# Loads at the changes of pair in product order, h ahead of w_out, and the two heads' value products side by side

## The chip, the cores and the metric

One core of a Trainium2 chip. The metric is device time in microseconds (us) of one launch. TensorE does the matmuls, VectorE and ScalarE the elementwise work, GpSimd little; SyncE (SP) issues all the large transfers, on one queue and in program order. Each engine works through its own list in order and waits at semaphores for the others.

## The reference, cut to what matters

4096 tokens of width 1024, one layer, all float32:

```
proj = x @ w_in                       # 1024 -> 3584 columns
xa, ba, ca, u, v, xc, da, dg, q, gate = split(proj)
y_a = ba * conv3(ca * xa)             # short gated convolution
y_b = spatial_gating(u, v)
y_c = multiscale_pool(xc)
y_d = silu(layer_norm(conv31(da * sigmoid(dg)))) @ w_pw
k, v = split(mem @ w_kv)              # 256 memory rows, 4 heads of 64
y_e = softmax(q k^T / 8) v            # per head
h = concat(y_a .. y_e) * silu(gate)   # width 1280
x = layer_norm(alpha * x + h @ w_out)
```

## The kernel before, in words

**Tiling.** The 4096 tokens are eight blocks of 512, worked as four pairs. For each pair (`p`) the input projection makes all 3584 columns, in 14 sets that `mpair` (L226) computes one after the other; between them stand the five branches, whose results are multiplied by their gates and written to DRAM as `h`. After the fourth pair comes the output stage: 32 chunks of 128 tokens, `h @ w_out` and the layer norm (the loop near the end, matmuls at L758).

**Products.** `mpair` computes a 2x2 block product (two blocks of tokens by two chunks of columns, the inner dimension in two halves) by seven products in place of eight: PA, PT1, PT2, PB, PT3, PD, PT4, in this order. Their x side are seven sums and differences of the four quarters b11, b12, b22, b21 of the pair's x. Each is kept as a high and a low part, so that a product is 12 matmuls of 128x512: for k = 0 to 3 the low part by the high weights (L210), the high part by the low weights (L212), the high by the high (L213). Each x tile has two halves along k, `kap` 0 (k 0 and 1) and `kap` 1 (k 2 and 3), so a product needs both. The results go through PSUM banks `mm`; PT1's and PT2's are read by VectorE's adds `t` and `v` (L91), the later ones by the adds to `cc`. The sixth product, PD, needs a bank that the `t` add has read.

**x_prep** (L122) makes these 28 tiles, which have one place each: eight loads of 512 KB (`load`, L131) to `xraw`, eight subtractions in place (`sub`, L94), and for each of the fourteen halves `split_to`: ScalarE casts to the high part (L87), VectorE subtracts for the low part (L88). A tile of the next pair can be written when the last product of the old pair that reads its place is done. So the change of pair falls into the last `mpair` of the old pair and the first of the new one. For the first pair all eight loads are in flight at once. For the later pairs the code goes half by half: four loads of kap 0 and seven steps, then four loads of kap 1 and seven steps; all eight use the four `raw` slots, so that the loads of kap 1 wait for steps of kap 0.

**The filter.** The 31-tap convolution (`d_conv`, L463) of a pair is 60 steps on VectorE, on two accumulators, fed out bit by bit (`take`) while the next pair's first sets run. `d_tail` then takes the result; it begins with transposes on TensorE (L429).

**Attention** (`attention`, L599) runs 16 times: four pairs, two groups of heads (`i`), two blocks (`n`). Queries are cast (L594) and subtracted, scores for two heads `j` are made on TensorE (L608), the exponentials scaled, and each head's 128x512 is transposed in two parts `mc` (four transposes each, L628), copied out by ScalarE (L631, `pT`) and multiplied by the values (L633). A value product has 64 columns, one half of the array: head 0 writes partitions 0 to 63 of `po`, head 1 partitions 64 to 127.

**The last change.** After the fourth pair the 28 places of the x tiles are given out again, in the order in which the products free them (`free`, `place`). `w_out` comes as ten tiles of 512 KB (`woraw`, L706), each split into two places; then `lng` and `lnb`; and `htags`, the six places of `h`, are the last six. `load_h(0)` (loads at L726) loads and splits the first 256 rows of `h`.

**Order.** The program is written once in Python, and each engine's list, SP's too, is put in order by a scheduler.

Of the kernel before, what the change touches and what calls it, by code (L numbers as in the profile page):

```python
# [11 lines left out]
F32 = mybir.dt.float32  # L12
# [10 lines left out]
T = 512  # L23
# [4 lines left out]
NKO = DMIX // P  # L28
# [24 lines left out]
def trunk(ctx, tc, a, out):  # L53
    nc = tc.nc
# [10 lines left out]
    def nm(s):  # L65
        uid[0] += 1
        return f"{s}_{uid[0]}"
# [5 lines left out]
    def tt(tag, dt=F32, n=None):  # L73
        cols, bufs = SLOTS[tag]
        return (wp if tag == "ws" else tp).tile([P, cols], dt, tag=tag, name=nm(n or tag), bufs=bufs)
# [10 lines left out]
    def split_to(hi, lo, src):  # L86
        nc.scalar.copy(out=hi, in_=src)  # L87
        nc.vector.tensor_tensor(out=lo, in0=src, in1=hi.bitcast(F32), op=ALU.subtract)  # L88
# [4 lines left out]
    def sub(dst, x, y):  # L93
        nc.vector.tensor_tensor(out=dst, in0=x, in1=y, op=ALU.subtract)  # L94
# [27 lines left out]
    def x_prep(p):  # L122

        xs = [[None, None] for _ in range(7)]
        raws = {}

        def put(i, kap, src):
            xs[i][kap] = x_place(i, kap)
            split_to(*xs[i][kap], src)

        def load(kap, j, n):  # L131
            tag = "big" if p == 0 and kap == 1 else "raw"
            raw = tt(tag, n="xraw")[:, :2 * T].rearrange("p (k t) -> p k t", k=2)
            k0 = 4 * j + 2 * kap
            nc.sync.dma_start(out=raw, in_=a["xT"][:, k0:k0 + 2, (2 * p + n) * T:(2 * p + n + 1) * T])
            raws[kap, j, n] = raw

        def step(kap, i):
            b11, b12, b22, b21 = (raws.get((kap, *q)) for q in ((0, 0), (0, 1), (1, 1), (1, 0)))
            if i == PT1:  # L140
                sub(b11, b12, b11)
            elif i == PT2:
                sub(b11, b22, b11)
            elif i == PT3:
                sub(b12, b22, b12)
            elif i == PT4:
                sub(b21, b21, b11)
            put(i, kap, {PA: b11, PT1: b11, PT2: b11, PB: b21, PT3: b12, PD: b22, PT4: b21}[i])

        if p == 0:  # L150
            for q in ((0, 0), (0, 1), (1, 1), (1, 0)):
                for kap in range(2):
                    load(kap, *q)
                yield
            for i in range(7):
                for kap in range(2):
                    step(kap, i)
                yield
        else:
            for kap in range(2):  # L160
                for q in ((0, 0), (0, 1), (1, 1), (1, 0)):
                    load(kap, *q)
                for i in range(7):
                    step(kap, i)
        yield xs

# [168 lines left out]
    vm = const([P, 2, 256])  # L335
# [263 lines left out]
    def attention(p, i, n, src, g):  # L599
        q = queries(src)  # L600
        es = [tt("big", n="e")[:, :2 * T].rearrange("p (c m) -> p c m", c=NC4) for _ in range(2)]
        for c2 in range(2):
            sc = [bank(pa, "ax").rearrange("p (c m) -> p c m", c=2) for _ in range(2)]
            for c in range(2):
                t0 = (2 * c2 + c) * P
                for j in range(2):
                    for r, k in enumerate((k1, k2)):
                        nc.tensor.matmul(out=sc[j][:, c], lhsT=q[:, j, t0:t0 + P], rhs=k[i][:, j],  # L608
                                         start=(r == 0), stop=(r == 1))
            for j in range(2):  # L610
                mx = sp.tile([P, 2], F32, tag="mx", name=nm("mx"))
                nc.vector.tensor_reduce(out=mx, in_=sc[j], axis=AX.X, op=ALU.max, negate=True)  # L612
                e = es[j][:, 2 * c2:2 * c2 + 2]
                su = sp.tile([P, 2], F32, tag="su", name=nm("su"))
                for c in range(2):
                    nc.scalar.activation(out=e[:, c], in_=sc[j][:, c], func=AF.Exp, bias=mx[:, c:c + 1],  # L616
                                         accum_out=su[:, c:c + 1])
                ri = sp.tile([P, 2], F32, tag="ri", name=nm("ri"))
                nc.vector.reciprocal(out=ri, in_=su)
                for c in range(2):  # L620
                    nc.vector.tensor_scalar(out=e[:, c], in0=e[:, c], scalar1=ri[:, c:c + 1], scalar2=None,
                                            op0=ALU.mult)
        po = bank(pa, "ax")
        for j in range(2):
            for mc in range(2):
                pt = bank(pa, "ax")
                for c in range(NC4):
                    nc.tensor.transpose(out=pt[:, P * c:P * c + P], in_=es[j][:, c, P * mc:P * mc + P],  # L628
                                        identity=ident)
                pT = tt("wk", n="pT")[:, :T]  # L630
                nc.scalar.copy(out=pT, in_=pt)  # L631
                hd = 2 * i + j
                nc.tensor.matmul(out=po[64 * j:64 * j + 64], lhsT=vm[:, mc, 64 * hd:64 * hd + 64], rhs=pT,  # L633
                                 start=(mc == 0), stop=(mc == 1))
        nc.vector.tensor_tensor(out=g, in0=po, in1=g, op=ALU.mult)
        store(2 * p + n, 8 + i, g)

# [27 lines left out]
    for p in range(NPAIR):  # L665
# [15 lines left out]
        for i in range(2):  # L681
            q, ge = mpair(xs)
# [15 lines left out]
    free = [xc_tag for i in range(7) for kap in range(2) for s in "hl" for xc_tag in (f"x{i}{kap}{s}",)]  # L698

    def place(dt=F32R, n="wo"):  # L700
        return xc.tile([P, 2 * T], dt, tag=free.pop(0), name=nm(n))

    wo = []
    for k in range(NKO):
        raw = tt("raw", n="woraw")
        nc.sync.dma_start(out=raw, in_=a["w_out"][k])  # L706
        wo.append((place(), place()))
        split_to(*wo[k], raw)
    lng, lnb = place(F32, "lng"), place(F32, "lnb")
    nc.sync.dma_start(out=lng, in_=a["ln_g"])  # L710
    nc.sync.dma_start(out=lnb, in_=a["ln_b"])
    htags = free[:6]

    def load_h(u):

# [16 lines left out]
                for k in range(NKO)]  # L732

    hn = load_h(0)
    for b in range(NB):
        for c in range(NC4):
            r0 = b * T + c * P
            if c % 2 == 0:
                hh = hn
            elif r0 < SEQ - P:  # L740
                if r0 == (SEQ - 2 * T) - P:
                    take(conv, 60)
                    d_tail(NPAIR - 1, accs)
                hn = load_h((r0 + P) // 256)
            take(conv, 3)
            r = [tt("cc", n="r") for _ in range(2)]
            for n in range(2):
                nc.sync.dma_start(out=r[n], in_=a["x"][r0:r0 + P, T * n:T * n + T])
            st = sp.tile([P, 2, 6], F32, tag="st2", name=nm("st2"))
            ps = [bank(pm, "mm") for _ in range(2)]  # L750
            steps = [(n, k) for k in range(NKO) for n in range(2)]
            if r0 == SEQ - P:
                steps.sort()
            for n, k in steps:
                hi, lo = hh[k]
                whi, wlo = wo[k]
                for l, ww in ((lo, whi), (hi, wlo), (hi, whi)):
                    nc.tensor.matmul(out=ps[n], lhsT=l[:, P * (c % 2):P * (c % 2) + P], rhs=ww[:, T * n:T * n + T],  # L758
                                     start=(k == 0 and l is lo), stop=(k == NKO - 1 and ww is whi and l is hi))
            for n in range(2):  # L760
                nc.vector.scalar_tensor_tensor(out=r[n], in0=r[n], scalar=ALPHA, in1=ps[n],  # L761
                                               op0=ALU.mult, op1=ALU.add)
                nc.vector.bn_stats(out=st[:, n], in_=r[n])
            mv = sp.tile([P, 2], F32, tag="mv2", name=nm("mv2"))
            nc.vector.bn_aggr(out=mv, in_=st)
            rs = sp.tile([P, 1], F32, tag="rs2", name=nm("rs2"))
            rstd_of(rs, mv[:, 1:2], 1, EPS)
            for n in range(2):
                nc.vector.scalar_tensor_tensor(out=r[n], in0=r[n], scalar=mv[:, 0:1], in1=lng[:, T * n:T * n + T],
                                               op0=ALU.subtract, op1=ALU.mult)  # L770
                nc.vector.scalar_tensor_tensor(out=r[n], in0=r[n], scalar=rs, in1=lnb[:, T * n:T * n + T],
                                               op0=ALU.mult, op1=ALU.add)
                nc.sync.dma_start(out=out[r0:r0 + P, T * n:T * n + T], in_=r[n])
# [59 lines left out]
```

## Time and profile before

| what | value |
|---|---|
| median of 3 runs | 1776.53 us (1776.23 to 1777.87) |
| profiled execution, its own time | 1778.75 us |
| its span | 1777.0 us, mean granted clock 0.993 |
| TensorE busy (PE) | 1728.5 us, 97% |
| VectorE busy (DVE) | 1334.4 us, 75% |
| ScalarE busy (ACT) | 506.6 us, 29% |
| chain that ended last | PE 87%, DVE 7%, DMA 3% |

Busy time is the sum over an engine's instructions, as a share of the span. The chain is the work that ended last, followed back from the last instruction. The granted clock is the share of TensorE's full clock that the chip let it run at: 1.00 is 2.4 GHz, 0.50 is 1.2 GHz. Matmul records have modelled ends, so the distance from one start to the next tells more than the length of one: 0.227 us here for a 128x512 matmul.

### The profile page before, as it was taken

How to read it: one execution, taken by the hardware profiler on the slowest of the kernel's cores; microseconds unless marked ns; L12 is line 12 of the kernel's file. 1: busy time of each engine (PE TensorE's matmuls, PEld its weight loads, DVE VectorE, ACT ScalarE, POOL GpSimd, SP SyncE). 2: the span in 40 equal slices, each digit the busy share in tenths (PEclk: the TensorE clock that was granted, in tenths of full speed). 3: DMA queues.
4: the chain of work that ended last, by engine and by line, in shares of the span. 5: the costliest groups of instructions: out<-in, count | busy, mean ns of one | idle time of the engine just before them, and what ended most of it. 6: DMA issues, size and time to landing. Idle time of an engine off the chain costs nothing.

```text
span 1777.0 us, 21764 instructions
## 1 busy us (share of the span) xinstructions
PE 1728.5 (97%) x7912; PEld 1379.6 (78%) x7912; DVE 1334.4 (75%) x2461; ACT 506.6 (29%) x937; POOL 46.2 (3%) x87
## 2 busy tenths in 40 slices
PE   5999999989999999999999999999989999999997
PEld 4888777878877787887778788777868888888786
DVE  8678887799966539997653999766379996665765
ACT  4323644420144423013532411354241011000300
POOL 0000000000100001010000011000000000000000
PEclk9999999999999999999999999999999999999999
DMA  7767555776754467675446766544683344332621
GB/s 277 264 248 262 199 196 191 286 245 214 239 165 139 130 228 271 203 233 181 131 147 220 265 210 220 198 144 143 207 289 105 115 137 147 125 101 83 213 72 48
DMA packets 128091, 332.79 MB, mean 187 GB/s; under 512 B 14064, under 2 KB 36080, under 8 KB 127984
## 3 DMA queue, kind: packets, MB, share of 16 engines
q1 hardware_dynamic: 127984, 331.39, 55.1%
q8 instruction: 63, 1.03, 0.2%
q14 instruction: 44, 0.36, 0.1%
HBM read 238.02 MB, written 93.32 MB: 186 GB/s over the span
## 4 chain that ended last, share of the span: by engine, by line
PE 87%; DVE 7%; DMA 3%; issue 1%; ACT 1%; SPq 0%; DVEq 0%; ACTq 0%
PE mm L758 24%; PE mm L210 18%; PE mm L213 18%; PE mm L212 18%; PE ax L633 3%; DVE xl L88 2%; PE ax L608 2%; PE ax L628 2%; DVE xraw L94 2%; DMA xraw<-in_xT 1%; PE ax L578 1%; PE ax L429 1%; DVE w L88 1%; PE ax L486 0%; PE ax L476 0%
## 5 line engine op out<-in xcount | busy, mean ns | idle before, releaser
L210 PE MATMUL mm<-xl,w 128*128 128x512 f32 x1568 | 620.4, 396 | 27.5 <-DVE xl L88 21.3
L212 PE MATMUL mm<-xh,w 128*128 128x512 f32 x1568 | 617.2, 394 | 0.9 <-DVE w L88 0.9
L213 PE MATMUL mm<-xh,w 128*128 128x512 f32 x1568 | 615.9, 393 | 0.0
L758 PE MATMUL mm<-wo,h 128*128 128x512 f32 x1920 | 439.8, 391 | 7.5 <-DVE h L88 7.5
L758 PEld LDWEIGHTS mm<-wo,h 128*128 128x128 f32 x1920 | 361.1, 188 | 82.9 <-DVE h L88 8.4
L210 PEld LDWEIGHTS mm<-xl,w 128*128 128x128 f32 x1568 | 296.2, 189 | 94.8 <-DVE xl L88 26.6
L213 PEld LDWEIGHTS mm<-xh,w 128*128 128x128 f32 x1568 | 296.1, 189 | 63.5 <-issue 3.6
L212 PEld LDWEIGHTS mm<-xh,w 128*128 128x128 f32 x1568 | 296.5, 189 | 61.6 <-issue 2.5
L463 DVE SCALAR_TENSOR_TENSOR acc<-din,c,acc 128x1024 f32<-128x1024 f32 x240 | 304.5, 1284 | 0.6 <-ACT acc L460 0.2
L87 ACT CAST h<-hraw 128x1024 fp32r<-128x1024 f32 (+1 forms) x48 | 43.4, 911 | 314.6 <-PE mm L758 250.5
L91 DVE TENSOR_TENSOR cc<-mm,v 128x512 f32<-128x512 f32 x112 | 76.8, 688 | 61.7 <-PE mm L213 61.1
L761 DVE SCALAR_TENSOR_TENSOR r<-r,mm 128x512 f32<-128x512 f32 x64 | 43.5, 693 | 76.5 <-PE mm L758 76.4
L87 ACT CAST xh<-xraw 128x1024 fp32r<-128x1024 f32 x56 | 57.4, 1051 | 65.2 <-DVE xraw L94 43.3
L88 DVE TENSOR_TENSOR xl<-xraw,xh 128x1024 fp32r<-128x1024 f32 x56 | 66.7, 1222 | 11.6 <-ACT xh L87 11.6
L91 DVE TENSOR_TENSOR t<-mm,t 128x512 f32<-128x512 f32 x56 | 38.6, 689 | 46.7 <-PE mm L213 46.3
L389 ACT ACTIVATE cc<-cc 128x512 f32<-128x512 f32 x44 | 27.9, 634 | 152.5 <-DVE cc L91 152.3
L237 ACT COPY t<-mm 128x512 f32<-128x512 f32 x56 | 32.9, 588 | 123.8 <-PE mm L213 123.7
L88 DVE TENSOR_TENSOR h<-hraw,h 128x1024 fp32r<-128x1024 f32 (+1 forms) x48 | 50.0, 1047 | 24.1 <-ACT h L87 13.3
L612 DVE TENSOR_REDUCE mx<-ax 128x2 f32<-128x512 f32 x64 | 42.7, 682 | 30.1 <-PE ax L608 29.9
L91 DVE TENSOR_TENSOR cc<-mm,t 128x512 f32<-128x512 f32 x56 | 38.5, 688 | 34.7 <-PE mm L213 34.2
L616 ACT ACTIVATE e<-ax,mx 128x256 f32<-128x256 f32 x128 | 59.3, 477 | 17.1 <-DVE mx L612 16.2
L436 ACT ACTIVATE nrm<-ax,nmr,rs 128x256 f32<-128x256 f32 x64 | 30.7, 571 | 114.4 <-DVE nmr L434 114.4
(147 smaller groups left out, 1536.4 us busy)
## 6 DMA issues: line engine op xcount, KB each, us to landing
w<-wd SPq DMA_DIRECT2D x294, 512.0 KB, 3.8
wd<-w SPq DMA_DIRECT2D x98, 512.0 KB, 2.9
xraw<-in_xT SPq DMA_DIRECT2D x32, 512.0 KB, 5.4
h<-cc SPq DMA_DIRECT2D x64, 256.0 KB, 3.2
hraw<-h SPq DMA_DIRECT2D x32, 512.0 KB, 4.2
r<-in_x SPq DMA_DIRECT2D x64, 256.0 KB, 3.0
out<-r SPq DMA_DIRECT2D x64, 256.0 KB, 2.0
wraw<-in_w_in SPq DMA_DIRECT2D x22, 512.0 KB, 4.2
```

What stands on the lines that cost most here:

```text
L87: nc.scalar.copy(out=hi, in_=src)
L88: nc.vector.tensor_tensor(out=lo, in0=src, in1=hi.bitcast(F32), op=ALU.subtract)
L91: nc.vector.tensor_tensor(out=dst, in0=x, in1=y, op=ALU.add)
L210: nc.tensor.matmul(out=ps, lhsT=w[:, 0, k], rhs=xl[:, r], start=start and k == 0, stop=False, skip_group_check=True)
L212: nc.tensor.matmul(out=ps, lhsT=w[:, 1, k], rhs=xh[:, r], start=False, stop=False, skip_group_check=True)
L213: nc.tensor.matmul(out=ps, lhsT=w[:, 0, k], rhs=xh[:, r], start=False, stop=stop and k == 3, skip_group_check=True)
L463: nc.vector.scalar_tensor_tensor(out=accs[i], in0=dins[i][:, k:k + 2 * T], scalar=dww[:, i, k:k + 1], in1=accs[i], op0=ALU.mult, op1=ALU.add)
L612: nc.vector.tensor_reduce(out=mx, in_=sc[j], axis=AX.X, op=ALU.max, negate=True)
L616: nc.scalar.activation(out=e[:, c], in_=sc[j][:, c], func=AF.Exp, bias=mx[:, c:c + 1], accum_out=su[:, c:c + 1])
L633: nc.tensor.matmul(out=po[64 * j:64 * j + 64], lhsT=vm[:, mc, 64 * hd:64 * hd + 64], rhs=pT, start=(mc == 0), stop=(mc == 1))
L758: nc.tensor.matmul(out=ps[n], lhsT=l[:, P * (c % 2):P * (c % 2) + P], rhs=ww[:, T * n:T * n + T], start=(k == 0 and l is lo), stop=(k == N ...
L761: nc.vector.scalar_tensor_tensor(out=r[n], in0=r[n], scalar=ALPHA, in1=ps[n], op0=ALU.mult, op1=ALU.add)
```

## The change

It has three parts. In `x_prep` the pairs after the first load all eight tiles at once, in the order in which the products need them (b12, b11 of kap 0, b11, b12 of kap 1, then b22, then b21), and make the steps product by product with both halves; three of the kap 1 loads get `big` slots. In `attention` the loop over `mc` is now the outer one: both heads are transposed and copied, then both value products follow, and a dependence that no data asks for makes the first of them wait for the second head's copy. At the end `h` takes the first six places and is loaded ahead of `w_out`, which moves back, with `lng` and `lnb` last.

```diff
@@ -129,7 +129,7 @@
             split_to(*xs[i][kap], src)
 
         def load(kap, j, n):
-            tag = "big" if p == 0 and kap == 1 else "raw"
+            tag = "big" if kap == 1 and (p == 0 or (j, n) != (1, 0)) else "raw"
             raw = tt(tag, n="xraw")[:, :2 * T].rearrange("p (k t) -> p k t", k=2)
             k0 = 4 * j + 2 * kap
             nc.sync.dma_start(out=raw, in_=a["xT"][:, k0:k0 + 2, (2 * p + n) * T:(2 * p + n + 1) * T])
@@ -157,10 +157,11 @@
                     step(kap, i)
                 yield
         else:
-            for kap in range(2):
-                for q in ((0, 0), (0, 1), (1, 1), (1, 0)):
-                    load(kap, *q)
-                for i in range(7):
+            for kap, q in ((0, (0, 1)), (0, (0, 0)), (1, (0, 0)), (1, (0, 1)), (0, (1, 1)), (1, (1, 1)), (0, (1, 0)),
+                           (1, (1, 0))):
+                load(kap, *q)
+            for i in range(7):
+                for kap in range(2):
                     step(kap, i)
         yield xs
 
@@ -621,17 +622,23 @@
                     nc.vector.tensor_scalar(out=e[:, c], in0=e[:, c], scalar1=ri[:, c:c + 1], scalar2=None,
                                             op0=ALU.mult)
         po = bank(pa, "ax")
-        for j in range(2):
-            for mc in range(2):
+        for mc in range(2):
+            pTs, copies = [], []
+            for j in range(2):
                 pt = bank(pa, "ax")
                 for c in range(NC4):
                     nc.tensor.transpose(out=pt[:, P * c:P * c + P], in_=es[j][:, c, P * mc:P * mc + P],
                                         identity=ident)
-                pT = tt("wk", n="pT")[:, :T]
-                nc.scalar.copy(out=pT, in_=pt)
+                pTs.append(tt("wk", n="pT")[:, :T])
+                copies.append(nc.scalar.copy(out=pTs[j], in_=pt))
+            for j in range(2):
                 hd = 2 * i + j
-                nc.tensor.matmul(out=po[64 * j:64 * j + 64], lhsT=vm[:, mc, 64 * hd:64 * hd + 64], rhs=pT,
-                                 start=(mc == 0), stop=(mc == 1))
+                mm = nc.tensor.matmul(out=po[64 * j:64 * j + 64], lhsT=vm[:, mc, 64 * hd:64 * hd + 64], rhs=pTs[j],
+                                      start=(mc == 0), stop=(mc == 1))
+                if j == 0:
+                    tc.add_manual_dep(mm.ins, copies[1].ins.name,
+                                      mybir.DependencyInfo(mybir.DependencyClass.Sync, mybir.DependencyReason.DATA),
+                                      reason="both heads' products follow each other")
         nc.vector.tensor_tensor(out=g, in0=po, in1=g, op=ALU.mult)
         store(2 * p + n, 8 + i, g)
 
@@ -700,16 +707,7 @@
     def place(dt=F32R, n="wo"):
         return xc.tile([P, 2 * T], dt, tag=free.pop(0), name=nm(n))
 
-    wo = []
-    for k in range(NKO):
-        raw = tt("raw", n="woraw")
-        nc.sync.dma_start(out=raw, in_=a["w_out"][k])
-        wo.append((place(), place()))
-        split_to(*wo[k], raw)
-    lng, lnb = place(F32, "lng"), place(F32, "lnb")
-    nc.sync.dma_start(out=lng, in_=a["ln_g"])
-    nc.sync.dma_start(out=lnb, in_=a["ln_b"])
-    htags = free[:6]
+    htags = [free.pop(0) for _ in range(6)]
 
     def load_h(u):
 
@@ -732,6 +730,15 @@
                 for k in range(NKO)]
 
     hn = load_h(0)
+    wo = []
+    for k in range(NKO):
+        raw = tt("raw", n="woraw")
+        nc.sync.dma_start(out=raw, in_=a["w_out"][k])
+        wo.append((place(), place()))
+        split_to(*wo[k], raw)
+    lng, lnb = place(F32, "lng"), place(F32, "lnb")
+    nc.sync.dma_start(out=lng, in_=a["ln_g"])
+    nc.sync.dma_start(out=lnb, in_=a["ln_b"])
     for b in range(NB):
         for c in range(NC4):
             r0 = b * T + c * P
```

Line numbers of the new kernel are one higher from L130 to L620 (L464 is the old L463); the transposes are L630, the copies L633, the value products L636, the loads of `h` L724 and of `w_out` L736.

**VectorE, the change from pair 1 to 2**, from the first filter steps on. `xl` are the low parts, `xraw` the loads with their subtractions in place, `t_5921` the `t` add of the new pair's first set, `acc` the filter's steps, `din` its input. Before:

```order
L463 SCALAR_TENSOR_TENSOR acc_6036<-din_5694,c_225,acc_6036 128x1024
L463 SCALAR_TENSOR_TENSOR acc_6442<-din_5897,c_225,acc_6442 128x1024
L88 TENSOR_TENSOR xl_5871<-xraw_5857,xh_5870 128x1024
L94 TENSOR_TENSOR xraw_5859<-xraw_5861,xraw_5859 128x1024
L94 TENSOR_TENSOR xraw_5857<-xraw_5861,xraw_5857 128x1024
L88 TENSOR_TENSOR xl_5880<-xraw_5863,xh_5879 128x1024
L88 TENSOR_TENSOR xl_5885<-xraw_5859,xh_5884 128x1024
L88 TENSOR_TENSOR xl_5876<-xraw_5857,xh_5875 128x1024
L88 TENSOR_TENSOR xl_5889<-xraw_5861,xh_5888 128x1024
L94 TENSOR_TENSOR xraw_5863<-xraw_5863,xraw_5857 128x1024
L91 TENSOR_TENSOR t_5921<-mm_5938,t_5921 128x512
```

Now, up to the first filter step:

```order
L88 TENSOR_TENSOR xl_5884<-xraw_5827,xh_5883 128x1024
L88 TENSOR_TENSOR xl_5876<-xraw_5823,xh_5875 128x1024
L88 TENSOR_TENSOR xl_5866<-xraw_5831,xh_5865 128x1024
L94 TENSOR_TENSOR xraw_5829<-xraw_5829,xraw_5819 128x1024
L94 TENSOR_TENSOR xraw_5831<-xraw_5831,xraw_5821 128x1024
L451 SCALAR_TENSOR_TENSOR din_5897<-th_5898,cc_5815 128x512
L88 TENSOR_TENSOR xl_5889<-xraw_5829,xh_5888 128x1024
L451 SCALAR_TENSOR_TENSOR din_5897<-cc_5799,cc_5782 128x512
L88 TENSOR_TENSOR xl_5894<-xraw_5831,xh_5893 128x1024
L91 TENSOR_TENSOR t_5921<-mm_5938,t_5921 128x512
L464 SCALAR_TENSOR_TENSOR acc_6036<-din_5694,c_225,acc_6036 128x1024
```

All subtractions and splits now stand ahead of `t_5921`, and no filter step does; before, two filter steps stood ahead of it, and one split behind.

**TensorE, one attention step of pair 1** (group 0, block 0), its end: transposes of the probabilities `e` into a bank, value products from `pT`, and the score matmuls (`q`) of the next step. Ahead of the first row stand one value product (`pT_4693`) and eight transposes. Before:

```order
L628 MATMUL ax_4712<-c_188,e_4630 128x128 x2
L633 MATMUL ax_4687<-pT_4701,c_250 64x512
L633 MATMUL ax_4687<-pT_4709,c_250 64x512
L628 MATMUL ax_4712<-c_188,e_4630 128x128 x2
L608 MATMUL ax_4732<-c_246,q_4725 128x256
L608 MATMUL ax_4732<-c_248,q_4725 128x256
L608 MATMUL ax_4733<-c_246,q_4725 128x256
L608 MATMUL ax_4733<-c_248,q_4725 128x256
L608 MATMUL ax_4732<-c_246,q_4725 128x256
L608 MATMUL ax_4732<-c_248,q_4725 128x256
L633 MATMUL ax_4687<-pT_4717,c_250 64x512
```

Now, from the first value product on:

```order
L636 MATMUL ax_4687<-pT_4693,c_250 64x512
L636 MATMUL ax_4687<-pT_4700,c_250 64x512
L630 MATMUL ax_4704<-c_188,e_4629 128x128 x4
L630 MATMUL ax_4711<-c_188,e_4630 128x128 x4
L609 MATMUL ax_4732<-c_246,q_4725 128x256
L609 MATMUL ax_4732<-c_248,q_4725 128x256
L609 MATMUL ax_4733<-c_246,q_4725 128x256
L609 MATMUL ax_4733<-c_248,q_4725 128x256
L609 MATMUL ax_4732<-c_246,q_4725 128x256
L609 MATMUL ax_4732<-c_248,q_4725 128x256
L636 MATMUL ax_4687<-pT_4709,c_250 64x512
L636 MATMUL ax_4687<-pT_4716,c_250 64x512
```

The value products stood one, two, one; now they stand two and two, with eight transposes and six score matmuls between the pairs.

**ScalarE, the last change.** `wo` are the high parts of `w_out`, `h` those of the first 256 rows of `h`, `th`, `cc` and `acc` the last filter's input and start. Before, the end of the list:

```order
L87 CAST wo_11218<-woraw_11216 128x1024
L87 CAST wo_11224<-woraw_11222 128x1024
L87 CAST wo_11230<-woraw_11228 128x1024
L448 ACTIVATE cc_11155<-cc_11155 128x512
L87 CAST wo_11236<-woraw_11234 128x1024
L460 ACTIVATE acc_11261<-din_11058,c_231,c_225 128x1024
L460 ACTIVATE acc_12388<-din_11171,c_231,c_225 128x1024
L87 CAST h_11244<-hraw_11249 128x1024
L87 CAST h_11245<-hraw_11253 128x1024
```

Now, its beginning:

```order
L449 ACTIVATE cc_11040<-cc_11040 128x512
L87 CAST h_11181<-hraw_11189 128x1024
L87 CAST h_11180<-hraw_11185 128x1024
L238 COPY t_11082<-mm_11067 128x512
L87 CAST h_11184<-hraw_11193 128x512
L87 CAST wo_11199<-woraw_11197 128x1024
L87 CAST wo_11205<-woraw_11203 128x1024
L87 CAST wo_11211<-woraw_11209 128x1024
L449 ACTIVATE th_11172<-mm_11067 128x512
```

`h` has gone from behind the tenth `wo` tile to ahead of the first; VectorE's and SP's lists moved alike.

## Rows read from the trace of the kernel before

**Rows 1.** TensorE's waits, whole span: for whom, us in total, times, longest

```profile
PE mm L210 <- DVE xl L88: 21.3, 12, 7.4
PE mm L210 <- DVE t L91: 5.2, 3, 3.7
```

**Rows 2.** TensorE's waits in the first 60 us

```profile
PE mm L210 <- DVE xl L88: 13.0, 5, 7.4
PE mm L210 <- DVE t L91: 3.7, 1, 3.7
```

**Rows 3.** TensorE's waits at 340 to 375, 650 to 700, 1290 to 1325

```profile
PE mm L210 <- DVE xl L88: 4.5, 3, 2.9
...
PE mm L210 <- DVE xl L88: 1.9, 2, 1.5
PE mm L210 <- DVE t L91: 0.8, 1, 0.8
...
PE mm L758 <- DVE h L88: 6.8, 1, 6.8
PE mm L210 <- DVE cc L91: 0.9, 1, 0.9
```

**Rows 4.** Stretches: us, busy PE, PEld, DVE, ACT, POOL, then PEclk, DMA, GB/s

```profile
367.00:370.60 3.60, 3.60 (x11) 2.76 (x10) 3.02 (x3) 0.54 (x1) 0.00 (x0) 0.55 0.56 166
690.00:808.00 118.00, 117.23 (x518) 96.49 (x517) 116.63 (x133) 14.89 (x23) 10.37 (x14) 1.00 0.73 238
1320.00:1326.00 6.00, 5.99 (x20) 4.84 (x21) 6.00 (x6) 1.23 (x2) 0.00 (x0) 0.74 0.80 233
```

**Rows 5.** VectorE's groups, 657.5 to 690: busy us, mean ns, idle before

```profile
L88 DVE TENSOR_TENSOR xl<-xraw,xh 128x1024 fp32r<-128x1024 f32 x13 | 15.4, 1220 | 2.4 <-ACT xh L87 2.4
```

**Rows 6.** VectorE's timeline: start, us, line, operation, [idle before]

```profile
335.53 1.23 DVE L88 TENSOR_TENSOR xl<-xraw,xh 128x1024 fp32r<-128x1024 f32 x1 [0.45 <-ACT xh L87]
...
359.64 1.28 DVE L463 SCALAR_TENSOR_TENSOR acc<-din,c,acc 128x1024 f32<-128x1024 f32 x1
...
364.26 4.63 DVE L88 TENSOR_TENSOR xl<-xraw,xh 128x1024 fp32r<-128x1024 f32 x4
...
657.66 1.23 DVE L88 TENSOR_TENSOR xl<-xraw,xh 128x1024 fp32r<-128x1024 f32 x1 [1.03 <-ACT xh L87]
...
678.87 2.47 DVE L463 SCALAR_TENSOR_TENSOR acc<-din,c,acc 128x1024 f32<-128x1024 f32 x2
...
690.34 0.68 DVE L91 TENSOR_TENSOR t<-mm,t 128x512 f32<-128x512 f32 x1
...
806.33 1.29 DVE L463 SCALAR_TENSOR_TENSOR acc<-din,c,acc 128x1024 f32<-128x1024 f32 x1
```

**Rows 7.** TensorE's timeline: first matmuls of pairs 1 and 2, filter's transposes

```profile
352.60 0.39 PE L210 MATMUL mm<-xl,w 128*128 128x512 f32 x1
...
674.05 0.39 PE L210 MATMUL mm<-xl,w 128*128 128x512 f32 x1
...
807.98 0.82 PE L429 MATMUL ax<-c,acc 128*128 128x128 f32 x6
```

**Rows 8.** SP's timeline, last change; the page's DMA issues (us to land)

```profile
1298.82 9.68 SPq L706 DMA_DIRECT2D woraw<-in_w_out  x5
...
hraw<-h SPq DMA_DIRECT2D x32, 512.0 KB, 4.2
```

**Rows 9.** The chain of waits, two attention steps of pair 1: start, us

```profile
543.12 1.00 PE ax L633 x2
...
545.39 1.56 PE ax L633 x4
...
547.32 0.72 PE ax L608 x6
...
558.80 0.60 ACT pT L631
```

**Rows 10.** ScalarE's timeline in the first of them

```profile
542.85 0.62 ACT L594 CAST q<-cc 64x512 fp32r<-64x512 f32 x1
```


## The prediction

> **What bounds the kernel now.** TensorE is busy 97% of the span, VectorE 75% (the table above), so only what keeps TensorE from starting its next matmul can be won. I read TensorE's waits first, then the stretches they lie in, then VectorE and the copies there. Over the whole span TensorE waits 21.3 us for VectorE's splits of x and 5.2 us for its `t` adds [rows 1]. 13.0 and 3.7 of that belong to the first 60 us [rows 2], whose branch of `x_prep` the edit leaves alone. What is left lies at four places [rows 3]: 4.5 us at the change from pair 0 to 1 (from here change 1), 1.9 + 0.8 at change 2, by difference as much (1.9 and 0.7) at change 3, and 6.8 + 0.9 at the last change, from projection to output. The 6.8 is one wait for `h`.
>
> Two waits cost more than their length. After the longest wait at change 1, 2.9 us [rows 3], the granted clock is 0.55 for 3.6 us, near the 1.2 GHz level; after the 6.8 us it is 0.74 over 6 us [rows 4]. Taken as lost time that is 3.6 x 0.45 = 1.6 and 6 x 0.26 = 1.6 us. Four places thus hold 6.1 + 2.7 + 2.6 + 9.3 = 20.7 us; beside them stand 16 attention steps, each with four value products.
>
> **Change 1.** Before, the kap 1 tiles were made last, and every product needs both halves. Now the eight loads and fourteen splits run in product order, so the walk over VectorE's order decides. It does 14 subtractions at L88, 1.22 us each by the mean [rows 5], and 8 of the same shape at L94; back to back they start 1.15 apart (four took 4.63, [rows 6]), which makes 22 x 1.15 = 25.3. Nine narrow operations of the last product set and the filters' input lie between them, 0.62 each, 5.6. From the first split at 335.53 [rows 6] that gives 366.4; with 0.4 for gaps and 0.7 for the `t` add, which the new order puts behind all of them, `t` is done at 367.5. TensorE comes to the new pair at 352.60 [rows 7]. It needs `t` before the sixth product, since that product's bank is freed by it: 60 matmuls x 0.227 = 13.6 later, at 366.2. So a wait of about 1.4 remains, now for `t`. The splits themselves are all in time; the tightest is PB's second half, whose load comes last and leaves 1.2 us by the same walk. Gain: 6.1 - 1.4 = **4.7**. Ends: 6.1 if `t` slips forward, nothing if the last load is late and VectorE, which works in order, stands behind it.
>
> **Changes 2 and 3.** The same walk with seven narrow operations: 657.66 [rows 6] + 25.3 + 4.3 + 0.4 + 0.7 = 688.4. TensorE enters at 674.05 [rows 7] and is due at the sixth product at 687.7. A wait of 0.7 stays, 2.0 go, twice: **4.0**. Ends: 0 and 5.3.
>
> **What the new order pushes back.** At change 2 the first steps of the 60-step filter stood at 678.87, at change 1 at 359.64 [rows 6]; now they stand behind `t`. From 690 to 808 VectorE is busy 116.6 of 118 us [rows 4], the last filter step starts at 806.33 [rows 6], ends 1.29 later, and TensorE's transposes of the result follow at 807.98 [rows 7], 0.4 us behind its end: almost a tie. What counts is not when the filter starts but when VectorE's sum of work is done, and that sum is unchanged. At change 2 VectorE now reaches the end of `t` 2.6 us earlier (it started at 690.34, [rows 6]), with two steps (2.5) more and one split (1.2) less ahead of it, so it ends 1.3 earlier. TensorE comes 2.0 earlier, and its transposes stand nine matmuls (2.05 us) later in pairs 2 and 3: no new wait. In pair 1 they move by one matmul only, TensorE is 4.7 earlier and VectorE 3.3 to 4.5: I take **-0.5** (0 to -1.5).
>
> **The last change.** `h` was last on SP, behind w_out: five w_out loads take 9.68 us to issue [rows 8], and `h` took the places that the last product frees. Now it takes places free from the first products, with its three loads ahead. The w_out tiles move three loads back; the last three take the positions of `h`, issued from 1309.6 on. With 4.2 us to land [rows 8] and about 2.3 for the split they are there by 1320. Each k feeds 6 matmuls (1.37 us), so from a start at 1313 the tenth is needed at 1325.5 and the eighth at 1322.8: some 5 us of slack. So 6.8 and 1.6 go; the 0.9 for `cc` [rows 3] comes from a split that stands ahead of it on VectorE and waits for a load; loads and splits there keep their positions, and I keep it. Gain **8.4**. Ends: 6.8 if the clock falls anyway, 9.3 if the 0.9 goes too.
>
> **Attention.** A value product alone takes 1.00 us, two adjacent ones on the two halves of the array 1.56 [rows 9]. Before, an attention step had one, two, one: 3.56. Now two and two: 3.12. Saved 0.44 x 16 = 7.0. Against it stands the added dependence: the first product waits for the second head's copy, and what is queued behind it on TensorE waits too. From the last transpose to a product it takes 0.04 + 0.60 for the copy [rows 9] + some 0.2 for the weight load: 0.85. At the first pair four to six matmuls (0.9 to 1.4 us) lie in between, which covers it, except where ScalarE has a `q` cast of 0.62 [rows 10] between the two copies: four times about 0.3. At the second pair it is mostly six score matmuls, 0.72 to 0.9 [rows 9], one of which needs the bank that the first copy frees: some 0.1 or less each. Less the few such waits that exist today I count 1.5 in all. Gain **5.5**. Ends: 7.0, or nothing (rival A).
>
> **Sum.** 4.7 + 4.0 - 0.5 + 8.4 + 5.5 = 22.1. The sum belongs to the profiled execution, 1778.75 us (span 1777.0), which stands 2.2 above the median of the runs, so it becomes 1756.6 there and **1754.4** on the median's footing. All bounds together at their best, 20.7 + 7.0 = 27.7, give 1748.8.
>
> **Rivals.** (A) The pairing gives nothing: the dependence costs what the adjacency saves, 0.44 an attention step. Then 1754.4 + 5.5 = 1759.9. For it: before, the second transposes hid the first copy, and now six matmuls have to; it decides if the wait reaches 0.22 at each pair. Against: the gaps above are 0.1 where they are tight. The Trainium skill (TensorE: Matmul & The Clock Gate, Part 3, The mechanism) holds that matmuls start and end strictly in program order, so that nothing overtakes a waiting product; by it every such gap costs its full length.
>
> (B) The changes of pair stay as they are: one late load stops VectorE and the wait changes only its name, from split to `t`. That loses 8.7: 1763.1. For it: VectorE's walk ends behind TensorE at all three. Against: it is behind by 0.7 to 1.4 only, where TensorE stood 2.7 and 6.1.
>
> (C) Both heads run wholly beside each other. Two adjacent products would then take 1.00 instead of 1.56: 32 x 0.56 = 18 more, 1736.5. Against: today's adjacent pair is already on two halves and takes 1.56 [rows 9]. The Trainium skill (same page, Part 3, Measured speedup vs the span model) has products on different column tiles overlap almost fully; by that rule the time is this rival's, and the row speaks against it.
>
> (D) Slower: the filter becomes the bound. It starts 7.9 us later at change 1 and 9.5 later at changes 2 and 3; should these 26.9 us come out at the transposes, less 2 x 2.05 for their later position, with 1.6 of slow clock at each, the price is 27.6: 1782. It is slower from 7.4 us a change on. Against: VectorE has no idle time there that a later start could lose, only an order. That the edit doesn't do what it says is excluded: in the new instruction order all 32 pairs of products are adjacent, and `h` is ahead of w_out on every queue.
>
> **Numbers.** My own case gets 0.73, A and B 0.10 each, C 0.03, D 0.04. My case alone runs from 1748 to 1761; with A and B inside, and without C and D, the range is 1748 to 1763. A measurement here can tell some 0.2%, 3.6 us, from no change: all but D lie beyond it, and a D at part of its price would be no change. So faster 0.94, same 0.02, slower 0.04.
>
> **What would show it.** In the profile after: TensorE's waits for x splits outside the first 60 us gone, in their place a wait for `t` of about 1.4 and twice 0.7; no wait for `h` near 1313 and no clock under 1.00 behind it; the 0.9 for `cc` still there; in the chain two pieces of 1.56 for each attention step and no piece of 1.00; TensorE waiting at most 1.5 at the filter's transposes in pair 1. I would be wrong if the waits for splits persist at changes 2 and 3, if the paired products show waits of 0.2 or more for the copies, or if output matmuls wait for w_out.

## The result, and the profile after

The changed kernel takes **1732.62 us** (median of 4 runs, 1731.49 to 1735.13) against 1777.2 of the kernel before in the same comparison (4 runs, 1776.23 to 1779.03): ratio 0.975, 95% interval 0.9733 to 0.9767, 44.6 us less. Forecast were 1754.4 and a range of 1748 to 1763. The sign was right and the size half of what came. The profiled span is 1731.9 us, 45.1 below the 1777.0 of before.

TensorE's waits after, over the whole span, then at 0 to 60, 340 to 375 and 1240 to 1290:

```profile
PE mm L211 <- DVE xl L88: 12.4, 5, 7.5
PE mm L211 <- DVE t L91: 4.8, 2, 3.6
PE mm L765 <- DVE h L88: 1.3, 1, 1.3
...
PE mm L211 <- DVE xl L88: 12.4, 5, 7.5
PE mm L211 <- DVE t L91: 3.6, 1, 3.6
...
PE mm L211 <- DVE t L91: 1.2, 1, 1.2
...
PE mm L211 <- DVE cc L91: 0.5, 1, 0.5
```

All 12.4 us for splits of x lie in the first 60 us, where the edit does nothing. The waits at the changes of pair [rows 3] are gone but for 1.2 us on `t` at change 1. The 6.8 for `h` is gone too; the 1.3 that remains is a wait of the same kind in the output stage, 0.7 before. The clock behind the last change, and its row of before [rows 4]:

```profile
1276.00:1282.00 6.00, 6.00 (x29) 4.95 (x28) 6.00 (x7) 4.64 (x6) 1.20 (x1) 1.00 0.97 352
```

In the main this is as forecast. To see where the 45.1 us came from, take ScalarE's one `t` copy in each set of products (L237, now L238). Two sets follow each other at 19.04 us when nothing disturbs them. Change 2 before, in ScalarE's timeline: the first set of the new pair takes 22.80, the next 19.04.

```profile
676.97 0.59 ACT L237 COPY t<-mm 128x512 f32<-128x512 f32 x1 [0.76 <-PE mm L213]
...
699.77 0.59 ACT L237 COPY t<-mm 128x512 f32<-128x512 f32 x1 [8.27 <-PE mm L213]
...
718.81 0.59 ACT L237 COPY t<-mm 128x512 f32<-128x512 f32 x1 [0.43 <-PE mm L213]
```

After, the same first set takes 19.35:

```profile
658.67 0.59 ACT L238 COPY t<-mm 128x512 f32<-128x512 f32 x1 [2.90 <-PE mm L214]
678.02 0.59 ACT L238 COPY t<-mm 128x512 f32<-128x512 f32 x1 [8.92 <-PE mm L214]
```

Done for all 56 copies in both timelines, the gain by stretch is:

| stretch (from copy to copy) | before ends at | after ends at | gain, us | forecast |
|---|---|---|---|---|
| start, to the second set | 67.18 | 65.46 | 1.7 | 0 |
| pair 0, with four attention steps | 336.37 | 329.05 | 5.6 | 1.4 |
| change 1 | 380.88 | 368.04 | 5.5 | 4.7 |
| pair 1 | 657.93 | 639.63 | 5.5 | 1.4 - 0.5 |
| change 2 | 699.77 | 678.02 | 3.45 | 2.0 |
| pair 2 | 976.76 | 949.21 | 5.8 | 1.4 |
| change 3 | 1018.66 | 987.60 | 3.5 | 2.0 |
| pair 3 | 1295.73 | 1259.02 | 5.65 | 1.4 |
| last change and output | 1777.0 | 1731.9 | 8.4 | 8.4 |

Each pair's gain comes between its seventh and its twelfth copy, where the attention steps stand: 22.5 us in all, against 5.5. TensorE's groups show it too. The value products of before, then of after:

```profile
L633 PE MATMUL ax<-pT,c 128*64 128x512 f32 x128 | 59.0, 617 | 0.9
```

```profile
L636 PE MATMUL ax<-pT,c 128*64 128x512 f32 x128 | 34.5, 618 | 0.3
```

The same 128 instructions, each as long as before, keep TensorE busy for 24.5 us less: they lie over each other. (A value product shows as two records of TensorE, so x2 is one product and x4 a pair.) In the chain, the step that corresponds to [rows 9]:

```profile
529.45 0.59 ACT pT L633
530.04 0.02 issue
530.06 0.62 ACT q L595
530.68 0.02 issue
530.70 0.59 ACT pT L633
531.30 0.04 issue
531.34 1.08 PE ax L636 x4
532.42 1.02 PE ax L630 x8
533.45 0.98 PE ax L609 x6
534.42 1.01 PE ax L636 x4
```

A pair of products takes 1.0, not 1.56: as long as one alone. That is rival C. The cast of `q` between the two copies, feared in the forecast, is there as well. Why the adjacent pair of before took 1.56 stands in ScalarE's copies and TensorE's weight loads at [rows 9], before:

```profile
544.75 1.07 ACT L631 COPY pT<-ax 128x512 f32<-128x512 f32 x2 [1.28 <-PE ax L628]
...
545.39 0.19 PEld L633 LDWEIGHTS ax<-pT,c 128*64 128x64 f32 x2 [0.26 <-ACT pT L631]
545.88 0.19 PEld L633 LDWEIGHTS ax<-pT,c 128*64 128x64 f32 x2 [0.30 <-ACT pT L631]
```

and after:

```profile
531.34 0.20 PEld L636 LDWEIGHTS ax<-pT,c 128*64 128x64 f32 x4 [0.53 <-ACT pT L633]
...
534.35 0.20 PEld L636 LDWEIGHTS ax<-pT,c 128*64 128x64 f32 x4
```

Before, the weights of the pair's two products were loaded 0.49 us apart, and the second product waited for its own copy: ScalarE makes the two copies one behind the other, 1.07 for both and 0.59 for one, so that they end 0.48 apart. The 1.56 of the chain is the 1.0 of a pair that starts together and the half us by which the second started late, printed as one piece of TensorE.

### The profile page after: what moved, and what is told of

The parts are those of the page before. It is cut to its first block, busy times and chain, and to the rows that moved or that the text cites. A ratio compares the mean times of both kernels' runs of the same rounds, so it can differ in the third digit from the quotient of the medians.

```text
span 1731.9 us, 21800 instructions
## 1 busy us (share of the span) xinstructions
PE 1699.8 (98%) x7912; PEld 1370.3 (79%) x7912; DVE 1331.4 (77%) x2461; ACT 505.5 (29%) x937; POOL 47.7 (3%) x87
## 4 chain that ended last, share of the span: by engine, by line
PE 90%; DVE 6%; ACT 2%; DMA 1%; issue 1%; SPq 0%; DVEq 0%; ACTq 0%
PE mm L765 24%; PE mm L214 19%; PE mm L211 19%; PE mm L213 19%; PE ax L636 2%; PE ax L609 2%; PE ax L630 2%; DVE xl L88 1%; DVE xraw L94 1%; PE ax L579 1%; PE ax L430 1%; ACT e L617 1%; DVE w L88 1%; PE ax L487 1%; PE ax L477 0%
## 5 line engine op out<-in xcount | busy, mean ns | idle before, releaser
L211 PE MATMUL mm<-xl,w 128*128 128x512 f32 x1568 | 620.1, 396 | 17.7 <-DVE xl L88 12.4
L464 DVE SCALAR_TENSOR_TENSOR acc<-din,c,acc 128x1024 f32<-128x1024 f32 x240 | 303.4, 1275 | 0.3
L238 ACT COPY t<-mm 128x512 f32<-128x512 f32 x56 | 32.9, 587 | 185.5 <-PE mm L214 175.1
L617 ACT ACTIVATE e<-ax,mx 128x256 f32<-128x256 f32 x128 | 59.2, 474 | 13.4 <-DVE mx L613 12.4
L633 ACT COPY pT<-ax 128x512 f32<-128x512 f32 x64 | 36.1, 589 | 46.3 <-PE ax L630 45.8
```

The costliest lines, as they stand in the source:

```text
L211: nc.tensor.matmul(out=ps, lhsT=w[:, 0, k], rhs=xl[:, r], start=start and k == 0, stop=False, skip_group_check=True)
L464: nc.vector.scalar_tensor_tensor(out=accs[i], in0=dins[i][:, k:k + 2 * T], scalar=dww[:, i, k:k + 1], in1=accs[i], op0=ALU.mult, op1=ALU.add)
L633: copies.append(nc.scalar.copy(out=pTs[j], in_=pt))
```

## The experiments

**Theory**: a value product holds TensorE for 1.00 us; two on different halves of the array take 1.0 together, provided that the second one's data are there when the first starts; the added dependence sees to that. **Rivals**: the pairs gain only with the other parts of the change; the overlap is of adjacent products wherever they lie; the exchanged loops do it and the dependence only costs.

**e1, the attention part alone.** The kernel before with

```diff
-        for j in range(2):
-            for mc in range(2):
+        for mc in range(2):
+            pTs, copies = [], []
+            for j in range(2):
...
+                if j == 0:
+                    tc.add_manual_dep(mm.ins, copies[1].ins.name,
```

> The kernel before with the attention part of the change alone. Theory: a value product alone holds TensorE for 1.00 us, and two on different halves of the array together take 1.0 too, if the second one's copy is there when the first starts; the 1.56 of the kernel before contained a wait of 0.5 for that copy. Then an attention step goes from 3.56 to some 2.1 whatever the other parts do: 16 x 1.4 = 22.6 less, 1754.6 us. Rival: the short pairs come only with the other parts, and alone the pairs stay at 1.56: 16 x 0.44 = 7 less, 1770.

Measured: 1754.48 us against 1777.43 (ratio 0.9866, 0.9848 to 0.9883), 22.9 less. Its pairs take 1.01 in the chain:

```profile
537.20 1.01 PE ax L635 x4
538.21 1.02 PE ax L629 x8
...
540.21 1.01 PE ax L635 x4
```

The theory's number; the first rival falls. By the copies of `t` its stretches with attention gain 23.4, the start gains 1.5, and the changes of pair lose 1.9.

**e2, the load order alone.**

```diff
-            tag = "big" if p == 0 and kap == 1 else "raw"
+            tag = "big" if kap == 1 and (p == 0 or (j, n) != (1, 0)) else "raw"
...
+            for i in range(7):
+                for kap in range(2):
                     step(kap, i)
```

> The kernel before with the new load order at the changes of pair alone. Theory: the gains between the sets of products, 5.5 + 3.45 + 3.5 = 12.5 us, belong to this part: 1764.7 us. Rival: only the waits that the profile lists are won, less the one that stays for t, 4.7 + 2.0 + 2.0 = 8.7: 1768.5.

Measured: 1766.73 (0.9936, 0.9921 to 0.9951), 10.7 less, between the two. In its trace the three changes give 5.0, 3.4 and 3.1, 11.5 in all, by the same copies as above: nearer the theory. 1.6 goes missing at the last change, where this kernel still waits 6.8 us for `h`, and 1.1 is won at the start, which the part leaves alone. The granted clock of the first 10 us of output, in the stretches of before and of e2:

```profile
1320.00:1330.00 10.00, 9.99 (x38) 8.14 (x39) 9.00 (x9) 2.62 (x3) 0.00 (x0) 0.84 0.88 287
```

```profile
1307.50:1317.50 10.00, 9.95 (x31) 7.96 (x32) 9.53 (x10) 2.62 (x3) 0.00 (x0) 0.69 0.85 280
```

After a wait of the same length the clock was lower over these 10 us; e1 shows 0.69 there as well, after a wait of 6.5. What such a wait costs through the clock differs between these profiles by 0.15 x 10 = 1.5 us, an estimate from the two rows.

**e3, h ahead of w_out alone.**

```diff
-    htags = free[:6]
+    htags = [free.pop(0) for _ in range(6)]
...
     hn = load_h(0)
+    wo = []
+    for k in range(NKO):
```

> The kernel before with h ahead of w_out alone. Theory: 6.8 us of waiting and 1.6 of slow clock go, 8.4: 1768.8 us. Rival: the clock falls anyway or w_out is late, 6.8 or less: 1770.4 or more.

Measured: 1767.49 (0.9945, 0.9925 to 0.9966), 9.9 less. The interval, 6 to 13 us, holds both ends. The profile favours the theory: no wait of TensorE between 1225 and 1320, not even the 0.9 for `cc`, and full clock behind the change; its last stretch gains 10.0, somewhat more than the 8.4:

```profile
1308.50:1314.50 6.00, 6.00 (x28) 4.97 (x27) 6.00 (x7) 4.92 (x5) 1.18 (x1) 1.00 0.87 287
```

The three parts alone give 22.9 + 10.7 + 9.9 = 43.5 us, together 44.6: they add up within the noise.

**e4, the changed kernel without the dependence.** The four lines of `add_manual_dep` are out.

> The changed kernel without the added dependence between the first product and the second head's copy. In the instruction order 25 of the 32 pairs stay adjacent and 7 are parted by a transpose. Theory: each parted pair costs a second 1.0 us (+7), and adjacent ones start as soon as the first copy is there, so that the second waits up to 0.5 for its own (0 to +12); what the first waits less is given back. Together 1737 to 1752 us, with pieces of 1.5 in the chain. Rival: adjacency alone does it and the dependence only costs: 1732 or less.

Measured: 1755.5 (ratio to before 0.9869, 0.9853 to 0.9885), 22.9 more than the changed kernel: the whole gain of the attention part, more than I had counted (1752 at most). Its chain has pairs of 1.56 and 2.07 and parted products of 1.0:

```profile
538.73 2.07 PE ax L636 x4
540.80 1.02 PE ax L630 x8
541.82 0.24 PE ax L609 x2
542.06 1.56 PE ax L636 x4
```

The 1.56 is back, in pairs that are adjacent in the order. So adjacency is not enough: a first product that starts as soon as it can makes the second wait alone. In the trace 28 of the 32 second products start 0.05 us after the end of their own copy. In the 25 adjacent pairs they start 0.09 to 1.07 behind the first, 14.7 us in all, where I had allowed 12 at most.

The dependence does this mostly through TensorE's list. In the changed kernel 25 of the 32 pairs start 0.12 us or more after the second copy's end, so that the copy no longer holds them, and in every pair TensorE does two to seven other matmuls between the end of the first copy and the pair's start. In the step shown above (first copy done at 530.04, pair at 531.34) they are matmuls of the projection:

```profile
530.16 0.39 PE L211 MATMUL mm<-xl,w 128*128 128x512 f32 x1
...
530.86 0.39 PE L211 MATMUL mm<-xl,w 128*128 128x512 f32 x1
```

In e4, 22 of the 32 first products have no such matmul ahead of them. The order of the changed kernel without the wait itself was not run.

The exchanged loops by themselves give nothing: e2 and e3 together would leave 1777.4 - 20.6 = 1756.8.

**e5, both products on the same half.** Head 1 adds into head 0's partitions (`start` and `stop` are moved to fit).

```diff
-                mm = nc.tensor.matmul(out=po[64 * j:64 * j + 64], ...
+                mm = nc.tensor.matmul(out=po[:64], ...
...
-        nc.vector.tensor_tensor(out=g, in0=po, in1=g, op=ALU.mult)
+        nc.vector.tensor_tensor(out=g[:64], in0=po[:64], in1=g[:64], op=ALU.mult)
```

> The changed kernel with both heads' value products on the same half of the array: head 1 adds into head 0's partitions, and only these 64 are multiplied by the gate (head 1's result and the other half of the gate's product are left out). Theory: the overlap needs different halves, so a pair takes 2.0 in place of 1.03: 32 x 1.0 = 31 us more, 1764. Rival: adjacent products overlap wherever they lie, the 1.03 is only the pipeline of one behind the other: 1733.

Measured: 1759.8, 27.2 more than the changed kernel (ratio to before 0.9898, 0.9883 to 0.9912). A pair now takes 1.86 to 1.93 in the chain; from the pair's start to that of the matmul behind it, it is 1.86 in 29 of the 32 pairs, and in the other three different matmuls lie between:

```profile
539.58 1.93 PE ax L636 x4
541.51 1.02 PE ax L630 x8
...
543.52 1.86 PE ax L636 x4
```

32 x (1.86 - 1.01) = 27.2. By the copies of `t` the stretches with attention take 26.1 more than in the changed kernel. Same adjacency, same dependence, same copies: it is the two halves that let the products overlap. Within a half the two only share 0.14. The run also puts both results in one place; that the adding costs the time is unlikely, since the projection's matmuls add into one bank twelve times over and follow each other at 0.227 throughout, but two products on one half with results in two places were not run.

**e6, the loops of before with a dependence in the middle.** Head 0's second product waits for head 1's first copy.

```diff
+                if (j, mc) == (1, 0):
+                    tc.add_manual_dep(mm.ins, cp_.ins.name,
```

> The kernel before, loops as they were, with one added dependence: the second product of head 0 waits for the first copy of head 1, so that the middle pair starts with both copies there. In the instruction order all three later products then stand together (halves 0, 1, 1). Theory: the pair takes 1.0 in place of 1.56 and the third product 1.0, 3.0 an attention step in place of 3.56: 16 x 0.5 = 8 us less, minus new waits for the copies of up to 0.3 each, 1769 to 1774 us. Rival: 1.56 is what two adjacent products take; then the wait only costs: 1777 to 1785.

Measured: 1763.19 (0.9917, 0.9902 to 0.9932), 15.0 less, where the theory said 3 to 8. Three products now follow each other, on halves 0, 1, 1:

```profile
536.87 1.00 PE ax L637 x2
537.87 1.46 PE ax L628 x12
539.33 0.30 PE ax L608 x2
539.63 1.93 PE ax L637 x6
```

Three products in 1.93, so 1.00 + 1.93 = 2.93 a step in place of 3.56: 10.1 us, and the stretches with attention give 12.8 in its trace; where the other 2.7 come from was not traced. Another 3.1 lie at the start, where this profile ran at a higher clock than that of before (1.00 against 0.66 from 38 to 48 us). The 1.56 goes by a dependence alone, with the old loops: it held a late start. The direction is the theory's; the size is larger than its 8, and the waits I had subtracted do not show.

**v1, the second head's copy on VectorE.**

```diff
-                copies.append(nc.scalar.copy(out=pTs[j], in_=pt))
+                copies.append(nc.scalar.copy(out=pTs[j], in_=pt) if j == 0 else nc.vector.tensor_copy(out=pTs[j], in_=pt))
```

> The changed kernel with the second head's copy on VectorE in place of ScalarE. Theory: the two copies of a pair then run side by side and no query cast stands between them; the weight loads' waits for copies, 8.9 us in the changed kernel, fall to under 4, and the time by 2 to 5 us: 1728 to 1731. Rival: what lies between hides them already, or VectorE is late with its row maxima for the next step: 1732 to 1736.

Measured: 1732.81 (0.9744, 0.9728 to 0.976), as the changed kernel. No idle time of the weight loads is put down to a copy any more, and the attention stretches gain 23.6 where the changed kernel gains 22.5. So the 8.9 that I had read as waits for copies were worth 1.1: the weight loads of the value products are idle for 9.9 us in the changed kernel and still for 8.9 here, under other names, and only seven pairs of the changed kernel start within 0.06 of their second copy's end. The 1.1 is spent again at change 1 (4.2 in place of 5.5), where the listed waits are longer in this profile (first and third row, of TensorE's waits from 340 to 1290; the changed kernel has 1.2 for `t` and no split at change 1, and the second row lies at the last change):

```profile
PE mm L211 <- DVE t L91: 1.9, 1, 1.9
PE mm L211 <- DVE cc L91: 0.6, 1, 0.6
PE mm L211 <- DVE xl L88: 0.3, 1, 0.3
```

None of the versions run beats the changed kernel.

## Why the prediction was wrong in its size

**Attention: the step that failed.** The sum read "two adjacent ones on the two halves of the array 1.56", took that for the price of a pair and made 2 x 1.56 of the new step. The pair costs 1.01 when both start together; the 1.56 held the 0.49 by which the second started late. The saving is 3.56 - 2.02 = 1.54 a step, 24.6 in all, and 22.5 came. Of the 2.1 between, v1 puts 1.1 down to the copies (I had counted 1.5 for waits); the rest is open. Measured 22.5 against 5.5: this term alone is 17.0 of the 23.0 us by which the spans' difference exceeds the sum. Rival C had the right mechanism (1736.5, and the measured median is 1732.6) and got a chance of 0.03, on the ground that the old pair was "already on two halves". It was, but its second product had its own wait, and the chain of waits prints successive pieces of one engine and line as one. What tells are the starts of the weight loads beside the ends of ScalarE's copies. The rule of the Trainium skill (TensorE: Matmul & The Clock Gate, Part 3, Measured speedup vs the span model), set aside for the row, holds here: two products on different halves took 1.01 where one takes 1.00. The rule on program order cited beside rival A (the Trainium skill, same page, Part 3, The mechanism) bears on the same place: e4's second products waited up to 1.07 behind the first, and no matmul from behind them in the list filled that time.

**Changes of pair: mechanism right, sizes low by 0.8 + 1.4 + 1.5.** The splits no longer bound them, `t` took their place at change 1 with 1.2 (forecast 1.4; the terms of that sum give 1.3) and nowhere else. Two sizes were off. I took a wait for what its row says, 1.9 + 0.8 = 2.7 at change 2. The set there took 22.80 - 19.04 = 3.76. A row counts idle time from the modelled end of the matmul before, 0.39 after its start, though the next would have started after 0.227; and the first matmul after a wait takes 0.34 to the next (e.g. 366.67 to 367.01 in the timeline of before). Some 0.3 more for each of three waits, an estimate from these distances. And the 0.4 us of gaps in VectorE's walk, with which I left a wait of 0.7 at changes 2 and 3, did not occur: VectorE's `t` ends at 669.47 after 639.36, 30.1 us, against my 30.7.

**The filter: right.** It now starts behind `t`, as the order said, and TensorE's transposes at L430 do not wait for it in any pair; the 0.5 us I took off for a tie in pair 1 was not due. Rival D did not come.

**The last change: 8.4 forecast and 8.4 measured**, with small errors of both signs: the wait for `cc` fell from 0.9 to 0.5, the wait for `h` in the output stage grew by 0.6. So the agreement to 0.1 is in part luck: e2 and e1 show that the clock's part of it, 1.6 in the profile of before, can as well be 3 (10 us at 0.69).

**The start: 1.7 us that no part of the change made.** From 38 to 48 us the granted clock was 0.66 in the profile of before and 0.83 after; in e3, whose start is the same program too, 1.00. The time to the second set differs by up to 3.1 us among kernels that share it.

## What to carry to other kernels

An engine's piece in a chain of waits is not a price until the rows inside it are checked for waits of their own: look at when each weight load starts, and at what paces the operands. Two narrow products on different halves of TensorE's columns took 1.0 here plus the time from the start of the first to that of the second: with 0.49 between half the overlap is lost, with 1.07 all of it. So let the pair stand in the list where the operands of both are ready, with other work ahead of it; a dependence on the later operand brought that about here. And a wait of TensorE cost some 0.3 us beyond its row here, which counts where many short ones are to be removed.

## What the runs showed of the hardware

Two float32 products of 64 columns by 512 on different halves take 1.01 us together, one alone 1.00, two on the same half 1.86. Three on halves 0, 1, 1 take 1.93 in the chain. Two on different halves of which the second starts 0.49 late take 1.56 in the chain, and 2.07 when it starts 1.07 late. After waits of the same 6.8 us for `h` the granted clock over the next 10 us was 0.84 in one profile and 0.69 in another.
